# Three quarters of the first feed-forward product in 2x2 blocks, with seven block products for eight, and weight sums by accumulating DMAs

## The chip, the cores and the metric

The kernel runs on one core of a Trainium2 chip. The metric is device time in microseconds (us); the figure for the kernel before is the median of three runs. Five engines with a queue of instructions each matter here: PE (TensorE: matmuls, with weight loads of its own beside them), DVE (VectorE), ACT (ScalarE), POOL (GpSimd) and SP (SyncE, which here issues only DMAs). Each works through its own queue in order; an instruction that waits for another engine or for a transfer holds everything behind it on its engine.

## What is computed

Two layers run over 640 tokens (128 of a prompt, 512 of a sample) of width 1024. The layer's first part, a mixer of four branches, is not changed. Its second part is the feed-forward network:

```
h = _rmsnorm(x, g_pre_ffn) * (1 + sc2) + sh2
f = jnp.square(jax.nn.relu(h @ w_ff1)) @ w_ff2        # w_ff1: 1024 x 4096, w_ff2: 4096 x 1024
x = x + gt2 * _rmsnorm(f, g_post_ffn)
```

Shift, scale and gate (sh, sc, gt) come from `mod = SiLU(cond) @ w_ada + b_ada` for each layer, one set for the prompt and one for the sample.

## The kernel before

**Precision.** Every factor is split into a high part (rounded to the type that PE multiplies at full rate) and a low part (the rest), and a product is three matmuls: high by high, high by low, low by high (`mm3`). A raw weight tile `wr` (128x1024) is loaded by SP, its high part `wh` is a cast on ACT (L160), and its low part `wl` is a subtraction on DVE (L170) that needs `wh`. Each such tile is a unit; 132 units make a layer. `w_fetch` issues loads (three raw buffers), `w_pump` the casts up to three units ahead (four sets of `wh` and `wl`), `w_low` the subtractions.

**Stages.** The feed-forward network runs in four quarters of 1024 hidden columns. A quarter has two stages. In the first, 8 units of w_ff1 give 8 blocks of 128 hidden columns (tile `ff`): for each block and each half of the tokens (320), `ws_half` makes 8 x 3 = 24 matmuls of 320 columns, then ACT takes relu and square (L1121, L1122, the latter writes the high part `ghi`), and DVE squares and subtracts for the low part `glo` (L1123, L1124). In the second, `natural`, 8 units of w_ff2 multiply `ghi` and `glo` into the output `f` (tile `nat`), 240 matmuls of 512 columns, in two halves of four units; each unit serves all five tiles of 128 tokens.

**Order.** Nothing reorders the program: the code's order is the order of each engine's queue. After a chunk of matmuls, `tick(pe, dve)` adds the estimated PE time to a credit and takes the estimated DVE time off; while credit is left, it advances side jobs, the attention and convolution parts and `ada`, which makes the modulation vectors: per chunk (`ada_chunk`) eight loads `wa` issued by ACT into four buffers, 16 DVE operations on `acc` (L419, L421), two all-reduces over partitions on POOL (L433); for shift and scale, small POOL DMAs through DRAM follow (L443 `mrow`, L446 `mc`), for a gate, a product on DVE (L460). `tick` also lets one pending `wl` go (`w_low(1)`).

Of the kernel before, what the change touches and what calls it, by code (L numbers as in the profile page):

```python
# [12 lines left out]
L = 2  # L13
# [56 lines left out]
class Kernel:  # L70
# [35 lines left out]
    def add(self, name, gen, unit, steps):  # L106
        self.sides.append(Side(name, gen, self.l * N_UNITS + unit, steps))
# [31 lines left out]
    def w_init(self):  # L139
        self.w_dma = 0  # L140
        self.w_split = 0
        self.w_at = 0
        self.w_live = 0
        self.w_raw = {}
        self.w_raw_live = 0
# [3 lines left out]
    def w_pump(self, upto):
        nc = self.nc  # L150
        total = L * N_UNITS
        while self.w_split <= min(upto, total - 1) and self.w_live < N_SETS:
            i = self.w_split
            if i not in self.w_raw:
# [4 lines left out]
            lo = self.wp.tile([128, 1024], F32R, tag="wl", name=self.nm("wl"), bufs=N_SETS)  # L159
            nc.scalar.copy(hi, raw)  # L160
            self.w_set[i] = (hi, lo)
            self.w_late.append((i, raw, hi, lo))
            self.w_split += 1
            self.w_live += 1
# [11 lines left out]
    def w_fetch(self, upto):  # L176
        while self.w_dma <= min(upto, L * N_UNITS - 1):
            i = self.w_dma
            if self.w_raw_live >= N_RAW:
                break  # L180
            self.w_raw_live += 1
            raw = self.wp.tile([128, 1024], F32, tag="wr", name=self.nm("wr"), bufs=N_RAW)
            self.nc.sync.dma_start(raw, self.a["wu"][i])
            self.w_raw[i] = raw
            self.w_dma += 1

    def w_next(self):
# [3 lines left out]
        self.w_low(upto=i)  # L191
# [210 lines left out]
    def ada_chunk(self, l, ch, red):  # L402
# [4 lines left out]
        w = {}  # L407
        for k in range(-3, 8):
# [13 lines left out]
            yield 1.4  # L422
        if gate:
# [26 lines left out]
    def ada_gate(self, l, v, G):  # L450
        nc, a = self.nc, self.a
        for h in range(2):
# [3 lines left out]
            for c in range(2):  # L456
# [3 lines left out]
                nc.vector.tensor_tensor(G[c][:, s], red[c], gp, ALU.mult)  # L460
                yield 0.6
# [103 lines left out]
    def x_load(self, t, src, bufs=3):  # L565
# [5 lines left out]
    def natural(self, hi, lo, f, mode, ch=None):  # L571
# [5 lines left out]
        for n in range(2):  # L577
# [37 lines left out]
            for j in range(4):  # L615
                u, st = self.w_next()
                for t in range(NT):
# [5 lines left out]
                    self.tick(*NAT_TICK[j])  # L623
# [485 lines left out]

    def ffn(self, hi, lo, f, ch):  # L1110
        nc = self.nc
        for c in range(4):
# [31 lines left out]
    def run(self):  # L1144
# [3 lines left out]
        with tc.tile_pool(name="cp", bufs=1) as self.cp, tc.tile_pool(name="lp", bufs=1) as self.lp, \  # L1148
# [22 lines left out]
            for l in range(L):  # L1171
# [39 lines left out]
class Chain:  # L1211
# [180 lines left out]
```

## Time and profile before

| | |
|---|---|
| median of 3 runs (lowest to highest) | 2087.73 us (2086.01 to 2090.85) |
| profiled execution: its time; span from the first to the last instruction | 2086.46 us; 2084.5 us |
| PE busy | 2031.9 us (97%) |
| DVE busy | 1312.2 us (63%) |
| ACT busy | 786.5 us (38%) |
| POOL busy | 287.5 us (14%) |
| HBM read | 208.61 MB |
| mean granted clock of PE | 0.991 |

All times of the sum are taken from this one execution. Busy time counts what an engine executes; matmuls are pipelined, so PE can be busy and still be slower than its peak: the distance from one matmul's start to the next tells its real pace. Waits are found in the timeline as idle time before an instruction, with the engine that ended it. In part 2 of the page the span is cut in 40 slices; the feed-forward quarters lie at about 597 to 1057 us and 1623 to 2078 us.

### The profile page before, as it was taken

To read this page: it belongs to the slowest core of one execution; us is meant where nothing else is said; L and a number is where in the kernel's file an instruction comes from. 1 tells how busy PE (TensorE), PEld (TensorE's weight loads), DVE (VectorE), ACT (ScalarE), POOL (GpSimd) and SP (SyncE) were. 2 spreads that over 40 slices of the span, in tenths; PEclk is the share of its full clock that TensorE was granted. 3 is DMA by queue.
4 is the path that set the end of the run, shared out by engine and by line. 5 is a ranking of instruction groups with operands and counts; after the bars stand their busy time and mean duration, and the time that the engine had idled before them with its cause. 6 is when DMAs were issued, how large, how long until landed. Compare 5 with 4: busy or idle time off the path is not lost. (4 is left out here: it accounts for less than half of the span.)

```text
span 2084.5 us, 30672 instructions
## 1 busy us (share of the span) xinstructions
PE 2031.9 (97%) x12354; PEld 1884.3 (90%) x12354; DVE 1312.2 (63%) x2306; ACT 786.5 (38%) x1540; POOL 287.5 (14%) x214
## 2 busy tenths in 40 slices
PE   8999999999999999999999989999999999999998
PEld 4999999899889898989889989989998989989896
DVE  6777875687678385657776878667435863333344
ACT  5433445442353331313344334455324523223131
POOL 1302001013131123111240020100101211000000
PEclk9999999999999999999999999999999999999999
DMA  7331221233434244343534112112224342222232
GB/s 295 123 111 60 83 71 36 98 121 115 149 132 162 99 135 131 112 132 123 169 108 133 63 64 72 51 67 96 72 72 147 136 142 81 75 78 74 78 102 80
DMA packets 77934, 221.40 MB, mean 106 GB/s; under 512 B 11224, under 2 KB 12248, under 8 KB 77792
## 3 DMA queue, kind: packets, MB, share of 16 engines
q1 hardware_dynamic: 48736, 165.32, 23.0%
q10 hardware_dynamic: 27520, 54.03, 7.7%
q8 instruction: 96, 1.57, 0.3%
q0 software_dynamic: 1536, 0.10, 0.2%
q14 instruction: 46, 0.38, 0.1%
HBM read 208.61 MB, written 10.80 MB: 105 GB/s over the span
## 5 line engine op out<-in xcount | busy, mean ns | idle before, releaser
L170 DVE TENSOR_TENSOR wl<-wr,wh 128x1024 fp32r<-128x1024 f32 x264 | 346.6, 1316 | 211.4 <-ACT wh L160 210.2
L160 ACT CAST wh<-wr 128x1024 fp32r<-128x1024 f32 x264 | 274.1, 1045 | 367.8 <-PE nat L210 291.5
L213 PE MATMUL ff<-hlo,wh 128*128 128x320 f32 x1024 | 318.3, 311 | 4.0 <-DVE hlo L546 2.8
L212 PE MATMUL gp<-hhi,wh 128*128 128x320 f32 x1024 | 319.8, 312 | 0.8 <-ACT sg L1080 0.6
L214 PE MATMUL ff<-hhi,wl 128*128 128x320 f32 x1024 | 318.1, 311 | 1.3 <-DVE wl L170 1.3
L212 PE MATMUL ff<-hhi,wh 128*128 128x320 f32 x1024 | 318.2, 311 | 0.0
L213 PE MATMUL gp<-hlo,wh 128*128 128x320 f32 x1024 | 317.3, 310 | 0.0
L214 PE MATMUL gp<-hhi,wl 128*128 128x320 f32 x1024 | 317.2, 310 | 0.0
L209 PE MATMUL nat<-wl,ghi 128*128 128x512 f32 x640 | 252.5, 395 | 0.0
L210 PE MATMUL nat<-wh,glo 128*128 128x512 f32 x640 | 252.4, 394 | 0.0
L208 PE MATMUL nat<-wh,ghi 128*128 128x512 f32 x640 | 252.3, 394 | 0.0
L433 POOL PARTITION_ALL_REDUCE red<-acc x40 | 147.5, 3731 | 723.0 <-DVE acc L421 374.4
L213 PEld LDWEIGHTS ff<-hlo,wh 128*128 128x128 f32 x1024 | 193.4, 189 | 5.4 <-issue 3.4
L421 DVE SCALAR_TENSOR_TENSOR acc<-wa,silu_c,acc 128x512 f32<-128x512 f32 x280 | 195.9, 758 | 2.6 <-DMA wa<-in_wada_dram 2.6
L212 PEld LDWEIGHTS gp<-hhi,wh 128*128 128x128 f32 x1024 | 193.1, 189 | 2.4 <-ACT sg L1080 0.9
L214 PEld LDWEIGHTS ff<-hhi,wl 128*128 128x128 f32 x1024 | 193.6, 189 | 1.8 <-DVE wl L170 1.8
L213 PEld LDWEIGHTS gp<-hlo,wh 128*128 128x128 f32 x1024 | 193.0, 189 | 1.1
L212 PEld LDWEIGHTS ff<-hhi,wh 128*128 128x128 f32 x1024 | 193.4, 189 | 0.4
L214 PEld LDWEIGHTS gp<-hhi,wl 128*128 128x128 f32 x1024 | 192.9, 188 | 0.1
L1080 ACT ACTIVATE sg<-gp 128x320 f32<-128x320 f32 x128 | 55.4, 434 | 288.4 <-PE gp L214 244.3
L1123 DVE TENSOR_TENSOR r<-r 128x320 f32<-128x320 f32 x128 | 62.6, 489 | 156.7 <-ACT ghi L1122 156.5
L1121 ACT ACTIVATE r<-ff 128x320 f32<-128x320 f32 x128 | 55.9, 437 | 248.0 <-PE ff L214 239.8
(205 smaller groups left out, 3803.6 us busy)
## 6 DMA issues: line engine op xcount, KB each, us to landing
wr<-in_wu_dram SPq DMA_DIRECT2D x264, 512.0 KB, 3.2
wa<-in_wada_dram ACTq DMA_DIRECT2D x160, 256.0 KB, 3.0
wa<-in_wada_dram SPq DMA_DIRECT2D x16, 512.0 KB, 8.8
x<-x ACTq DMA_DIRECT2D x15, 512.0 KB, 2.7
x<-x SPq DMA_DIRECT2D x15, 512.0 KB, 6.0
x<-in_x_sample_dram SPq DMA_DIRECT2D x8, 512.0 KB, 9.9
gp<-in_g_post_dram ACTq DMA_DIRECT2D x16, 256.0 KB, 3.2
out_dram<-x SPq DMA_DIRECT2D x10, 256.0 KB, 2.0
```

What stands on the lines that cost most here:

```text
L160: nc.scalar.copy(hi, raw)
L170: self.nc.vector.tensor_tensor(lo, raw, r32(hi), ALU.subtract)
L208: mm(out, lhsT=xhi, rhs=whi, start=start, stop=False)
L209: mm(out, lhsT=xhi, rhs=wlo, start=False, stop=False)
L210: mm(out, lhsT=xlo, rhs=whi, start=False, stop=stop)
L212: mm(out, lhsT=whi, rhs=xhi, start=start, stop=False)
L213: mm(out, lhsT=whi, rhs=xlo, start=False, stop=False)
L214: mm(out, lhsT=wlo, rhs=xhi, start=False, stop=stop)
L421: nc.vector.scalar_tensor_tensor(acc[c], w[k], s, acc[c], ALU.mult, ALU.add)
L433: nc.gpsimd.partition_all_reduce(red[c], acc[c], 128, bass_isa.ReduceOp.add)
L1121: nc.scalar.activation(r, ps[:, :HALF], AF.Relu)
L1123: nc.vector.tensor_tensor(r, r, r, ALU.mult)
```

## The change

In the quarters 1 to 3 of both layers (not in quarter 0) `ffn` calls `ffn_pairs` in place of the 16 `ws_half`. The product is cut in 2x2 blocks: the 1024 input features in two halves, two neighbouring blocks of 128 hidden columns as a pair, and the tokens in two halves of 320. Seven block products of 4 x 3 = 12 matmuls of 320 columns (tile `ffp`) replace the eight of a pair; there are four pairs in a quarter, so 28 block products. They run in the order 7, 1, 2, 6, 5, 3, 4 (`PRODUCTS`).

Each block product has a weight of its own, 128x512, half a set: product 1 uses W11 and 5 uses W11+W12, made in buffer X; 7 uses W12+W22, 6 the same with W11 added, 4 the same with W21 added too, made one after the other in buffer Y; 2 and 3 use W21 and W22 (buffer Z, a `wr` tile). X and Y live in the four `wa` buffers. SP loads the first block; every further one is added by a DMA that POOL issues with `accum_op=ALU.add` (`w_sum`): Y+W22 as soon as Y is loaded (`w_fetch`), the others behind the `wl` subtraction that still reads the old sum (`w_low`). A pair has four such DMAs. Casts run five block products ahead (`w_pump(None, base + i + 5)`).

Sums of activations are made once a layer by `ffn_acts`, as a side job in the second stage of quarter 0: for four k, 14 DVE operations of 320 columns and 4 ACT casts. After the products, DVE and ACT combine the seven results in two tiles U and R (128x640), and make `ghi` and `glo` of them 640 wide.

While X or Y are alive, `ada_chunk` does not start (`yield 0`); before a quarter's first X is loaded, an open chunk is run to its end at one go (`while self.ada_open`). Then `natural` without a chain ticks by `FF_TICK`, the `x` tiles have four buffers, and the chain asks for its scale and shift later (`late`). In all, PE has 288 matmuls fewer (6 x 48) and POOL 96 DMAs more.

```
+FF0 = 68
+PRODUCTS = [(p, n) for p in range(4) for n in (7, 1, 2, 6, 5, 3, 4)]
+_ALL, _LEFT, _RIGHT = slice(0, 512), slice(0, 512), slice(512, 1024)
+SOURCE = {1: ("X", _ALL, "12"), 5: ("X", _ALL, None), 7: ("Y", _ALL, "11"), 6: ("Y", _ALL, "21"), 4: ("Y", _ALL, None),
+          2: ("Z", _LEFT, "keep"), 3: ("Z", _RIGHT, None)}
+FF_TICK = ((1.39, 0), (1.39, 0), (1.39, 0), (1.39, 0.7))
...
+    def w_pump(self, upto, part=None):
+        while self.w_split < len(self.parts):
+            i, c, key, rc, then = self.parts[self.w_split]
+            if (i > upto or key[0] != "u" and i > self.w_at) if part is None else self.w_split > part:
+                break
...
                 self.w_low()
-            self.w_fetch(i)
-            raw = self.w_raw.pop(i)
-            hi = self.wp.tile([128, 1024], F32R, tag="wh", name=self.nm("wh"), bufs=N_SETS)
...
+            nc.scalar.copy(hi, raw[:, rc])
...
     def w_low(self, n=None, upto=None):
 
         while self.w_late and (n is None or n > 0) and (upto is None or self.w_late[0][0] <= upto):
-            i, raw, hi, lo = self.w_late.pop(0)
+            _, key, raw, hi, lo, then = self.w_late.pop(0)
             self.nc.vector.tensor_tensor(lo, raw, r32(hi), ALU.subtract)
-            self.credit -= W_DVE
-            self.w_raw_live -= 1
-            self.w_fetch(i + N_RAW)
+            self.credit -= W_DVE if key[0] == "u" else W_DVE / 2
+            if then in ("11", "12", "21", "22"):
+                self.w_sum(key, then)
+            elif then != "keep":
+                del self.w_raw[key]
+                self.w_raw_live["wa" if key[0] in "XY" else "wr"] -= 1
+            self.w_fetch()
...
+    def block(self, u, b):
+        return self.a["wu"][u + int(b[1]) - 1][:, (int(b[0]) - 1) * 512:int(b[0]) * 512]
+    def w_sum(self, key, b):
+        self.nc.gpsimd.dma_start(self.w_raw[key], self.block(key[1], b), accum_op=ALU.add)
...
+    def w_fetch(self, upto=None):
+        while self.w_dma < len(self.loads) and (upto is None or self.w_dma <= upto):
+            key = src, u = self.loads[self.w_dma]
+            pool = "wa" if src in "XY" else "wr"
+            if self.w_raw_live[pool] >= (4 if src in "XY" else N_RAW):
                 break
-            self.w_raw_live += 1
-            raw = self.wp.tile([128, 1024], F32, tag="wr", name=self.nm("wr"), bufs=N_RAW)
-            self.nc.sync.dma_start(raw, self.a["wu"][i])
-            self.w_raw[i] = raw
+            if src == "X":
+                if self.pair_set.get(u, 0) > self.w_at + 1:
+                    break
+                while self.ada_open:
+                    next(self.side_ada.gen)
+            self.w_raw_live[pool] += 1
+            if pool == "wa":
+                raw = self.ap.tile([128, 512], F32, tag="wa", name=self.nm("wx"), bufs=4)
+                self.nc.sync.dma_start(raw, self.block(u, "11" if src == "X" else "12"))
+            else:
+                raw = self.wp.tile([128, 1024], F32, tag="wr", name=self.nm("wr"), bufs=N_RAW)
+                if src == "u":
+                    self.nc.sync.dma_start(raw, self.a["wu"][u])
+                else:
+                    for i, b in enumerate(("21", "22")):
+                        self.nc.sync.dma_start(raw[:, i * 512:i * 512 + 512], self.block(u, b))
+            self.w_raw[key] = raw
+            if src == "Y":
+                self.w_sum(key, "22")
             self.w_dma += 1
 
...
         acc = [self.ap.tile([128, 512], F32, tag=f"acc{c}", name=self.nm("acc"), bufs=1) for c in range(2)]
         gate = ch // 2 in (2, 5)
         w = {}
+        while any(k[0] in "XY" for k in self.w_raw):
+            yield 0
+        self.ada_open = True
...
-                    self.tick(*NAT_TICK[j])
+                    self.tick(*(NAT_TICK if ch else FF_TICK)[j])
...
+    def ffn_acts(self, hi, lo, S):
...
+            def fin(f, x):
+                nc.scalar.copy(x[0], f)
+                v(x[1], f, r32(x[0]), ALU.subtract)
+            for f, x, y in ((f1, a21, a22), (f3, a11, a21)):
+                v(f, x[0], y[0], ALU.subtract)
+                v(f, f, x[1], ALU.add)
+                v(f, f, y[1], ALU.subtract)
+                yield 1.5
+            v(f2, f1, a11[0], ALU.subtract)
+            v(f2, f2, a11[1], ALU.subtract)
+            fin(f1, s1)
+            fin(f3, s3)
+            yield 2.0
+            v(f4, a12[0], f2, ALU.add)
+            v(f4, a12[1], f4, ALU.add)
+            fin(f2, s2)
+            fin(f4, s4)
+            yield 2.0

+    def ffn_pairs(self, hi, lo, S, ghi, glo):
+        nc = self.nc
+        v = nc.vector.tensor_tensor
+        p, q = slice(0, HALF), slice(HALF, NTOK)
+        acts = {1: [(hi[k][:, p], lo[k][:, p]) for k in range(4)], 2: [(hi[k][:, p], lo[k][:, p]) for k in range(4, 8)],
+                4: [(hi[k][:, q], lo[k][:, q]) for k in range(4, 8)], 3: S[4], 5: S[1], 6: S[2], 7: S[3]}
+        base = self.set_part[self.w_at]
+        late = []
+        for i, (pr, n) in enumerate(PRODUCTS):
+            self.w_pump(None, base + i + 5)
+            self.w_low(upto=base + i)
+            wh, wl = [w[:, (i % 2) * 512:(i % 2) * 512 + 512] for w in self.w_set[self.w_at]]
+            if n == 7:
+                U, R = self.T("u"), self.T("r")
+                p7 = self.sdps("ffp")
+            ps = (p7 if n == 7 else self.mmps("ffp"))[:, :HALF]
+            for k in range(4):
+                c = slice(k * 128, k * 128 + 128)
+                self.mm3(ps, wh[:, c], wl[:, c], *acts[n][k], k == 0, k == 3)
+            if n == 1:
+                nc.scalar.copy(U[:, p], ps)
+            elif n == 2:
+                v(R[:, p], ps, U[:, p], ALU.add)
+            elif n == 6:
+                v(U[:, p], ps, U[:, p], ALU.add)
+                v(R[:, q], p7[:, :HALF], U[:, p], ALU.add)
+            elif n == 5:
+                v(U[:, q], ps, R[:, q], ALU.subtract)
+                v(U[:, p], ps, U[:, p], ALU.subtract)
+            elif n == 3:
+                v(U[:, p], ps, U[:, p], ALU.add)
+                nc.scalar.activation(U, U, AF.Relu)
+                nc.scalar.activation(U, U, AF.Square)
+                nc.scalar.copy(ghi[2 * pr + 1], U)
+                late.append((2 * pr + 1, U))
+            elif n == 4:
+                v(R[:, q], ps, R[:, q], ALU.add)
+                nc.vector.scalar_tensor_tensor(R, R, 0.0, R, ALU.max, ALU.mult)
+                nc.scalar.copy(ghi[2 * pr], R)
+                late.append((2 * pr, R))
+            if late and n in (1, 2):
+                j, x = late.pop(0)
+                v(glo[j], x, r32(ghi[j]), ALU.subtract)
+            if i % 2:
+                self.w_free(self.w_at)
+                self.w_at += 1
+            self.tick(1.76, 1.4)
+        for j, x in late:
+            v(glo[j], x, r32(ghi[j]), ALU.subtract)
+        self.credit = 0.0
+        self.w_pump(self.w_at + SPLIT_AHEAD - 1)
...
-            order = [(i, h) for i in range(8) for h in range(2)]
-            if c == 0:
-                order = [(i, 0) for i in range(4)] + [(i, 1) for i in range(4)] + order[8:]
+            order = [(i, 0) for i in range(4)] + [(i, 1) for i in range(4)] + [(i, h) for i in range(4, 8) for h in range(2)]
+            if c:
+                self.drain("sums")
+                self.ffn_pairs(hi, lo, S, ghi, glo)
...
+            if c == 0:
+                self.add("sums", self.ffn_acts(hi, lo, S), FF0 + 14, 12)
...
         if self.ab:
-            self.A, self.B = self.k.make_ab(*self.ab)
+            self.k.need(*self.ab)
+            self.A, self.B = self.k.make_ab(*self.k.res[self.ab])
```

How the order changes is shown at three places of quarter 1 of the first layer. First ACT. Before, in the middle of the quarter's first stage, relu (`r`), square (`ghi`) and the casts `wh` of whole units:

```order
L1121 ACTIVATE r_1305_7623<-ff1_1302_7591 128x320
L1122 ACTIVATE ghi_1260_7412<-r_1305_7623 128x320
L1121 ACTIVATE r_1307_7655<-ff1_1306_7628 128x320
L1122 ACTIVATE ghi_1260_7412<-r_1307_7655 128x320
L160 CAST wh_1308_7662<-wr_1278_7446 128x1024
L1121 ACTIVATE r_1312_7695<-ff1_1310_7665 128x320
L1122 ACTIVATE ghi_1261_7413<-r_1312_7695 128x320
L1121 ACTIVATE r_1314_7725<-ff1_1313_7700 128x320
```

Now, from pair 0 to pair 1 (`wx_1271` is Y and `wx_1270` X of pair 1, `wr_1272` its Z; `wh_1311` left by product 6; `u` is U, `ffp_1320` is product 1 of pair 1):

```order
L202 CAST wh_1305_7586<-wr_1272_7460 128x512
L202 CAST wh_1311_7629<-wx_1271_7457 128x512
L1251 ACTIVATE u_1297_7532<-u_1297_7532 128x640
L1252 ACTIVATE u_1297_7532<-u_1297_7532 128x640
L1253 CAST ghi_1278_7509<-u_1297_7532 128x640
L202 CAST wh_1311_7629<-wx_1270_7455 128x512
L1258 CAST ghi_1277_7508<-r_1298_7533 128x640
L202 CAST wh_1315_7669<-wr_1272_7460 128x512
L202 CAST wh_1315_7669<-wx_1271_7457 128x512
L1240 COPY u_1317_7672<-ffp_1320_7690 128x320
```

A cast from Y now stands ahead of the copy of product 1 out of PSUM (last two rows): the copy comes behind the cast for product 4, whose source is the third sum in Y.

DVE before, the same stretch:

```order
L170 TENSOR_TENSOR wl_1309_7663<-wr_1278_7446,wh_1308_7662 128x1024
L1123 TENSOR_TENSOR r_1312_7695<-r_1312_7695 128x320
L1124 TENSOR_TENSOR glo_1269_7421<-r_1312_7695,ghi_1261_7413 128x320
L1123 TENSOR_TENSOR r_1314_7725<-r_1314_7725 128x320
L1124 TENSOR_TENSOR glo_1269_7421<-r_1314_7725,ghi_1261_7413 128x320
L170 TENSOR_TENSOR wl_1316_7731<-wr_1291_7521,wh_1315_7730 128x1024
L1123 TENSOR_TENSOR r_1320_7763<-r_1320_7763 128x320
L1124 TENSOR_TENSOR glo_1270_7422<-r_1320_7763,ghi_1262_7414 128x320
```

DVE now (from the `wl` of product 6 of pair 1 to the `wl` of product 7 of pair 2, `wx_1308`):

```order
L210 TENSOR_TENSOR wl_1312_7630<-wx_1271_7457,wh_1311_7629 128x512
L1262 TENSOR_TENSOR glo_1286_7517<-u_1297_7532,ghi_1278_7509 128x640
L210 TENSOR_TENSOR wl_1312_7630<-wx_1270_7455,wh_1311_7629 128x512
L1242 TENSOR_TENSOR r_1318_7673<-ffp_1324_7711,u_1317_7672 128x320
L1262 TENSOR_TENSOR glo_1285_7516<-r_1298_7533,ghi_1277_7508 128x640
L210 TENSOR_TENSOR wl_1316_7670<-wr_1272_7460,wh_1315_7669 128x512
L1244 TENSOR_TENSOR u_1317_7672<-ffp_1325_7728,u_1317_7672 128x320
L1245 TENSOR_TENSOR r_1318_7673<-ffp_1319_7674,u_1317_7672 128x320
L210 TENSOR_TENSOR wl_1316_7670<-wx_1271_7457,wh_1315_7669 128x512
L1247 TENSOR_TENSOR u_1317_7672<-ffp_1331_7755,r_1318_7673 128x320
L1248 TENSOR_TENSOR u_1317_7672<-ffp_1331_7755,u_1317_7672 128x320
L210 TENSOR_TENSOR wl_1323_7709<-wx_1308_7605,wh_1322_7708 128x512
```

The `wl` from `wx` stand between the operations that combine the products; the last one, which frees the next Y for its second sum, comes behind both that use product 5 (`ffp_1331`).

POOL before, around the start of the same quarter: two reductions, then two more, then the small DMAs.

```order
L433 ISA red_1249_7327<-acc_1213_7068 128x512
L433 ISA red_1253_7347<-acc_1214_7069 128x512
L433 ISA red_1318_7746<-acc_1284_7498 128x512
L433 ISA red_1322_7781<-acc_1285_7499 128x512
L443 DMA mrow_1327_7816<-red_1318_7746 16x1x32
L443 DMA mrow_1328_7817<-red_1322_7781 16x1x32
L446 DMA mc_1282_7496<-mrow_1327_7816 128x4x1
L446 DMA mc_1282_7496<-mrow_1328_7817 128x4x1
```

POOL now, from the last two reductions before the quarter (`red`) through pair 0 into pair 1 (`wx_1268` is Y of pair 0, `wx_1271` Y of pair 1, `wx_1308` Y of pair 2, `wx_1267` and `wx_1270` are X of pairs 0 and 1):

```order
L504 ISA red_1263_7437<-acc_1225_7086 128x512
L504 ISA red_1264_7439<-acc_1226_7087 128x512
L225 DMA wx_1268_7449<-in_wu_dram 128x512
L225 DMA wx_1271_7457<-in_wu_dram 128x512
L225 DMA wx_1268_7449<-in_wu_dram 128x512
L225 DMA wx_1267_7447<-in_wu_dram 128x512
L225 DMA wx_1268_7449<-in_wu_dram 128x512
L225 DMA wx_1308_7605<-in_wu_dram 128x512
L225 DMA wx_1271_7457<-in_wu_dram 128x512
L225 DMA wx_1270_7455<-in_wu_dram 128x512
L225 DMA wx_1271_7457<-in_wu_dram 128x512
```

The first addition to Y of pair 2 stands ahead of the second one of pair 1, and the first addition of all behind the two reductions. The load of `wx_1308` that it adds to is issued by SP when the `wl` of product 4 of pair 0 has read that buffer.

## Rows read from the trace of the kernel before

**Rows 1.** The page, part 1: busy time, share of the span, instructions.
```profile
PE 2031.9 (97%) x12354; PEld 1884.3 (90%) x12354; DVE 1312.2 (63%) x2306; ACT 786.5 (38%) x1540; POOL 287.5 (14%) x214
```

**Rows 2.** Windows: us, then busy us of PE, PEld, DVE, ACT, POOL; clock, DMA share.
```profile
720.00:770.00 50.00, 50.00 (x343) 50.00 (x342) 37.09 (x56) 19.57 (x35) 10.50 (x6) 1.00 0.42 139
776.00:826.00 50.00, 50.00 (x216) 40.42 (x215) 29.30 (x40) 7.36 (x7) 19.46 (x12) 1.00 0.38 120
1745.00:1795.00 50.00, 50.00 (x343) 50.00 (x342) 22.42 (x36) 19.69 (x36) 0.00 (x0) 1.00 0.22 74
```

**Rows 3.** Tile ff from 700 to 790 us: durations, first and last start.
```profile
L212 PE MATMUL ff<-hhi,wh x128: 309/309/310, 716.3 to 772.1; 128*128 128x320 f32 x128
```

**Rows 4.** Single lines on DVE and ACT: durations in ns, min/median/max.
```profile
L746 DVE TENSOR_TENSOR ptl<-PT,pth x60: 675/684/693, 133.8 to 1463.2; 128x512 fp32r<-128x512 f32 x60
...
L1016 DVE SCALAR_TENSOR_TENSOR ml<-macc,mh x16: 814/826/2896, 468.4 to 1566.8; 128x640 fp32r<-128x640 f32 x16
...
L543 ACT CAST hhi<-h x24: 406/620/626, 27.3 to 1637.6; 128x512 fp32r<-128x512 f32 x20, 128x256 fp32r<-128x256 f32 x4
...
L1015 ACT ACTIVATE mh<-macc x16: 728/732/741, 467.3 to 1566.0; 128x640 fp32r<-128x640 f32 x16
...
L1037 ACT COPY sb<-sec x8: 403/426/429, 123.4 to 1168.4; 128x320 f32<-128x320 f32 x8
```

**Rows 5.** Timeline of ACT, then of DVE: start us, us, line, operation, idle before.
```profile
1742.31 1.05 ACT L160 CAST wh<-wr 128x1024 fp32r<-128x1024 f32 x1
...
1743.40 1.23 DVE L170 TENSOR_TENSOR wl<-wr,wh 128x1024 fp32r<-128x1024 f32 x1 [5.63 <-ACT wh L160]
...
1750.37 0.49 DVE L1124 TENSOR_TENSOR glo<-r,ghi 128x320 fp32r<-128x320 f32 x1
1750.77 0.69 DVE L460 TENSOR_TENSOR G<-red,gp 128x512 f32<-128x512 f32 x1
```

**Rows 6.** DMA issues: KB each, median us from issue to landing.
```profile
wr<-in_wu_dram SPq DMA_DIRECT2D x264, 512.0 KB, 3.2
wa<-in_wada_dram ACTq DMA_DIRECT2D x160, 256.0 KB, 3.0
...
mc<-mrow POOLq DMA_DIRECT2D x24, 2.0 KB, 3.2
```

**Rows 7.** Spread of the landing: line L412 (wa), then tile mc.
```profile
DMA to landing us min/median/max: 2.5/3.0/5.3
...
DMA to landing us min/median/max: 2.5/3.2/5.0
```

**Rows 8.** Timeline of POOL: start us, us, line, operation.
```profile
998.04 7.91 POOL L433 PARTITION_ALL_REDUCE red<-acc  x2 [24.56 <-DVE acc L421]
...
1009.67 0.79 POOL L446 DMA_DIRECT2D mc<-mrow  x1 [2.81 <-DMA mrow<-red]
```

**Rows 9.** Timeline of DVE beside another such reduction on POOL.
```profile
963.79 0.49 DVE L1124 TENSOR_TENSOR glo<-r,ghi 128x320 fp32r<-128x320 f32 x1
964.20 3.26 DVE L170 TENSOR_TENSOR wl<-wr,wh 128x1024 fp32r<-128x1024 f32 x1
```

**Rows 10.** Timeline of PE at and behind two short waits.
```profile
1624.44 0.38 PE L213 MATMUL ff<-hlo,wh 128*128 128x320 f32 x1 [1.27 <-DVE hlo L546]
1625.48 0.64 PE L214 MATMUL ff<-hhi,wl 128*128 128x320 f32 x1 [0.66 <-DVE wl L170]
...
1628.32 0.47 PE L212 MATMUL ff<-hhi,wh 128*128 128x320 f32 x1
...
1628.83 0.31 PE L214 MATMUL ff<-hhi,wl 128*128 128x320 f32 x1
```

**Rows 11.** Window behind these waits, columns as in Rows 2.
```profile
1625.60:1628.60 3.00, 3.00 (x12) 3.00 (x13) 2.93 (x6) 0.06 (x1) 0.55 (x1) 0.50 0.63 190
```

**Rows 12.** The page, part 5: the sums of the modulation.
```profile
L421 DVE SCALAR_TENSOR_TENSOR acc<-wa,silu_c,acc 128x512 f32<-128x512 f32 x280 | 195.9, 758 | 2.6 <-DMA wa<-in_wada_dram 2.6
```

More of the change, by code (lines that the diff above doesn't have):

```diff
@@ L106, in add @@
     def add(self, name, gen, unit, steps):
-        self.sides.append(Side(name, gen, self.l * N_UNITS + unit, steps))
+        self.sides.append(Side(name, gen, self.set0[self.l] + unit, steps))
     def drain(self, *names):
@@ L139, in w_init @@
     def w_init(self):
+        self.parts, self.loads, self.set_part, self.set0, self.pair_set = [], [], [], [], {}
+        for l in range(L):
+            self.set0.append(len(self.set_part))
+            u = 0
+            while u < N_UNITS:
+                g = l * N_UNITS + u
+                if u < FF0 + 16 or (u - FF0) % 16:
+                    self.set_part.append(len(self.parts))
+                    self.parts.append((len(self.set_part) - 1, slice(0, 1024), ("u", g), slice(0, 1024), None))
+                    self.loads.append(("u", g))
+                    u += 1
+                    continue
+                for i, (p, n) in enumerate(PRODUCTS):
+                    if i % 2 == 0:
+                        self.set_part.append(len(self.parts))
+                        if i == 0:
+                            self.pair_set[g] = len(self.set_part) - 1
+                    src, cols, then = SOURCE[n]
+                    at = (i % 2) * 512
+                    self.parts.append((len(self.set_part) - 1, slice(at, at + 512), (src, g + 2 * p), cols, then))
+                self.loads += [(src, g + 2 * p) for p in range(4) for src in ("X", "Y", "Z")]
+                u += 8
+        self.set_part.append(len(self.parts))
         self.w_dma = 0
@@ L144, in w_init @@
         self.w_raw = {}
[L145 removed]
+        self.w_raw_live = {"wr": 0, "wa": 0}
         self.w_late = []
         self.w_set = {}
[L149 removed]
+        self.ada_open = False
+    def w_pump(self, upto, part=None):
         nc = self.nc
[L151 to L154, printed above, removed]
[L155 to L162 removed]
+        while self.w_split < len(self.parts):
+            i, c, key, rc, then = self.parts[self.w_split]
+            if (i > upto or key[0] != "u" and i > self.w_at) if part is None else self.w_split > part:
+                break
+            if i not in self.w_set:
+                if self.w_live >= N_SETS:
+                    break
+                self.w_set[i] = [self.wp.tile([128, 1024], F32R, tag=n, name=self.nm(n), bufs=N_SETS) for n in ("wh", "wl")]
+                self.w_live += 1
+            if key not in self.w_raw:
+                self.w_low()
+            while key[0] in "XY" and any(x[1] == key for x in self.w_late):
+                self.w_low(1)
+            self.w_fetch()
+            raw = self.w_raw[key]
+            hi, lo = [w[:, c] for w in self.w_set[i]]
+            nc.scalar.copy(hi, raw[:, rc])
+            self.w_late.append((self.w_split, key, raw[:, rc], hi, lo, then))
@@ L422, in ada_chunk @@
             yield 1.4
+        self.ada_open = gate
         if gate:
@@ L1110, in ffn @@
     def ffn(self, hi, lo, f, ch):
         nc = self.nc
+        S = {n: [] for n in range(1, 5)}
         for c in range(4):
```

33 lines of the change are left out of this document (22 added, 11 removed).

## The prediction

> **What bounds the kernel now.** I read the busy times first: PE is busy for 97% of the span, DVE for 63% [rows 1]. Busy is not yet bound, so next come windows inside the stages that change. In the first stage of a quarter 341 to 343 matmuls fit in 50 us, without a gap and at full clock; in the second stage 215 or 216 [rows 2]. So matmuls of 320 columns start 0.1466 us apart (50/341), those of 512 columns 0.2325 (50/215). A first stage begins at 716.3 and its last three matmuls at 772.1, with 3 x 128 = 384 matmuls [rows 3]: 56.3 us, which is 384 x 0.1466. So the stage is bound by the number of matmuls alone. DVE has 37 of 50 us there while modulation is made, 22 when it is not, ACT 20 [rows 2]. Then I read single operations [rows 4, 5], transfers [rows 6, 7], POOL [rows 8, 9] and the clock [rows 10, 11], because the change brings waits that this stage doesn't have.
>
> **What goes and what comes.** 48 matmuls fewer in each of six stages: 48 x 0.1466 = 7.0 us, 42 us in all; the floor of a stage is 28 x 12 x 0.1466 = 49.3 us. On DVE 8 `wl` (1.23 us) and 32 operations of 320 columns (0.49) go, 25.5 us; 28 half `wl` (0.68, as the operation of that shape in rows 4) and per pair seven operations of 320 and three of 640 (0.83) come: 19.0 + 4 x 5.9 = 42.7 us [rows 4, 5]. On ACT 28 half casts (0.62), and per pair a copy (0.43) and four of 640 (0.73): 31 us. Both would fit in 49.3 us, so neither is bound by its load. They are bound by their order, and that is what I price.
>
> **The chain in a pair.** Let x be the time from the end of the `wl` that frees Y to the moment at which the cast of the new sum can start: POOL's issue, transfer, landing. In ACT's order the cast for product 4 (third sum in Y) stands ahead of the copy of product 1. DVE's sums, and behind them the `wl` for 3, for 4, and for product 7 of the next pair, wait for that copy, and the next Y's second sum waits for this last `wl`. So one pair's third sum, which itself waits for the second, holds the next pair's second: a closed loop with two transfers in a row. POOL's order adds a third: Y+W22 of the pair after next stands ahead of the second sum of the next pair, and waits for a load into the buffer that product 4's `wl` has just freed. From the end of the `wl` for 4 to the same a pair later:
> load of Y, 2.7 us (256 KB land in 2.5 at the fastest, 3.0 in the middle [rows 6, 7]); POOL's issue of the addition, 0.8 [rows 8]; x; cast for 6 and its `wl`, 0.62 + 0.68 and two hand-overs of 0.04 (1743.36 to 1743.40 [rows 5]), 1.4; x; cast for 4 and the copy, 0.62 + 0.43, 1.1; on DVE a sum, a 640-wide `glo`, `wl` for 3, two sums, `wl` for 4, 0.49 + 0.83 + 0.68 + 0.98 + 0.68 less 5 x 0.09 overlap (1750.37 + 0.49 against 1750.77 [rows 5]), 3.2. Together 9.2 + 2x, where PE needs 84 x 0.1466 = 12.3.
>
> The quarter: the first pair's `wl` for 6 ends about 2.0 after the start (last evacuation 0.69 [rows 5], two half `wl`), then x, 1.1, and 2.5 on DVE: 5.6 + x. Two loops with the load in them: 18.4 + 4x. The last pair has none: 1.5 to its second sum, x, 1.4, x, 1.1, 1.8 on DVE, 5.8 + 2x; then PE still has 3.2 of block products 3 and 4. A stage takes **33.0 + 7x**, not under 49.3. It is even with 56.3 at x = 3.3.
>
> **The unknown x.** No transfer before adds to its target, and none from POOL is of this size. From below: a plain 256 KB load lands at the earliest 2.5 after its issue, and so does POOL's 2 KB `mc` [rows 7]. From above: `mc` has taken 5.0 and a `wa` load 5.3 [rows 7]; with the target read as well, 6. Between them: `mc` has 3.2 in the middle, and what 256 KB add is half of the 512 KB load (3.2) less the 256 KB load's fastest (2.5), 0.7 [rows 6, 7]. 3.2 + 0.7 = **3.9**, which I take: it is nearest to POOL's own row. Reading the target speaks for more (another 0.7), a quiet queue for less; traffic in these stages doubles (2 MB for 1 MB per pair), on queues that are busy for 0.22 to 0.42 before [rows 2]. At 3.9 a stage takes 60.3: 4.0 more, six times 24 us.
>
> **The starts.** Before quarter 1 of each layer a whole chunk of modulation and its two reductions stand ahead of the first `wl` on DVE and the first addition on POOL. The last unit's set comes free at half of the second stage (240 x 0.2325 = 55.8, so 27.9); cast and `wl` to 30.8, eight activation sums to 35, the chunk's loads 3 and seven steps of two operations (0.76 [rows 12]) to 47 or 48, the reductions 7.9 [rows 8]: 55.3. Y lands at 59.2, is cast at 59.9: PE starts about 4 late, and the second sum (`wl`, x, cast, `wl`) is 6 after the start where the sum above has 2: another 4. Twice 8 is 16. In quarters 2 and 3 of layer 0 the chunk runs earlier; the reductions end 5.6 before the start, the `wl` for 6 comes 5 after it, 3 late: 6 in all. In layer 1 there is no modulation left then. Beside a reduction DVE is held too: a `wl` of 1.23 takes 3.26 [rows 9]; the starts' estimate has that hidden, since DVE there waits for the same reductions. The 56 activation sums of a layer (27 us on DVE) lie in a second stage in which DVE has some 29 of 50 us [rows 2]; what they push back is in the start's 8.
>
> **The clock.** After waits of 1.27 and 0.66 us PE ran at the lower level: 12 matmuls in 3.0 us, so some 0.26 apart, at a granted clock of 0.50, before the higher one came back between 1628.3 and 1628.8 [rows 10, 11]. The 3.4 us from 1625.4 on at half pace cost 1.7. Inside a pair the chain hides it: from the release of 3 to the next pair's 6, PE has about 8.5 to do and the chain takes 9.7. Behind the last wait of a quarter nothing hides it: 6 x 1.7 = 10.
>
> **The sum.** 24 + 16 + 6 + 10 = 56 us on the profiled execution's own 2086.5: 2142.5. The median is 1.3 above that execution; I predict **2143**. As a rule in x: the total changes by 50x - 139 us, of which nought is at 2.8. Edits put at nothing: the fourth `x` buffer, the later request for scale and shift (hidden by a second stage in which DVE has 20 us to spare), the modulation chunks that move out of the first stages: if those no longer fit beside the second stages and the mixer, each costs up to its 11 us.
>
> The Trainium skill, page "DMA: Bandwidth & Descriptors", section "Anatomy of one DMA — SWDGE (gpsimd) path", fits a transfer from POOL as 2.0 us plus bytes over 436 GB/s. By it 256 KB take an estimated 2.6, and the sum would be rival A. This trace does not agree with its 2.0: 2 KB took 2.5 to 5.0 from POOL [rows 7].
>
> **Rivals.**
> A. The additions land like the fastest load, x = 2.6. Against it: only the fastest rows are so quick, and they move or read less. Then a stage takes 51.2, 5.1 less: -31, starts 2 x 5.4 + 2 x 0.4 = 12, no clock loss: **2068**. It decides below x = 2.8. Chance 0.14. By the fit of the Trainium skill above this is what would happen.
> B. The waits bind nowhere, x at or under 2.3 (say because the additions start moving before POOL's issue ends): -42 and 10 for the starts, **2055**. No row has a landing like that for a load. Chance 0.05.
> C. The additions queue behind the loads, x = 5: a stage takes 68, **2197**. For it: the spread of rows 7, and that 2 MB share the queues in a pair. Chance 0.15. The Trainium skill, same page, section "Issuing engines are not separate DMA queues", has all transfers interleave on the same 16 engines; the spread agrees.
> D. PE stays at the lower clock through these stages, because every pair has waits longer than those of rows 10: 28 x 12 x 0.26 = 87 us a stage, 31 more, **2271**. Against it: in 3.4 us without a wait it came back [rows 10]. Chance 0.03.
> That the change doesn't do what it says isn't one: 288 matmuls are gone from PE's order.
>
> **The numbers.** The forecast, x from 2.9 to 4.6, has 0.63: 2092 to 2178 (50x - 139 = 6 and 91). Faster by over 0.2%, about the smallest difference that a measurement tells from none: A and B, 0.19. Within it, x close to 2.8, off the forecast's lower end: 0.04. Slower: the rest of the forecast, C and D, 0.77. The range of 8 in 10 reaches down to A (2066) and up past C (2203): outside are B, D and the tails.
>
> **What would show it.** Right: PE's idle time before block products 6, 5 and 3, put down to `wh` and `wl` of the new tiles; ACT's casts from `wx` waiting for POOL's DMAs, and right behind them the copy of product 1 late by microseconds; first stages of some 60 us; landings of about 4 on POOL; the first stages of quarter 1 starting late. Wrong in size if landings are under 3; wrong in kind if the matmuls of a first stage follow each other at 0.147 without waits, or if PE waits for DVE at work rather than for transfers.

## The result, and the profile after

The changed kernel takes 2204.58 us (median of 4 runs, 2203.39 to 2206.72), the kernel before 2089.28 in the same comparison: ratio 1.0555, 95% interval 1.0537 to 1.0573. It is slower, as forecast, but by 115 us where 55 were forecast, and just above the range. The profiled execution has a span of 2201.6 us, 117.1 more than before.

Part 1 of the page answers to [rows 1]: PE has 288 matmuls fewer and a smaller share of the span; its busy time is longer all the same, which is due to its clock (below).

```profile
PE 2052.8 (93%) x12066; PEld 1877.5 (85%) x12066; DVE 1443.5 (66%) x2586; ACT 832.0 (38%) x1620; POOL 368.1 (17%) x310
```

Windows over the six changed stages, and over the two stretches ahead of the first quarter of each layer; columns as in [rows 2].

```profile
723.30:800.50 77.20, 62.58 (x337) 59.14 (x338) 38.62 (x66) 30.00 (x52) 13.22 (x15) 0.86 0.49 101
856.30:930.90 74.60, 59.50 (x338) 54.89 (x337) 37.97 (x66) 26.48 (x45) 12.36 (x15) 0.91 0.48 100
986.40:1060.60 74.20, 59.28 (x338) 54.79 (x337) 37.87 (x66) 26.42 (x45) 12.18 (x15) 0.91 0.49 101
1813.60:1889.30 75.70, 63.56 (x337) 59.49 (x338) 38.84 (x66) 29.85 (x52) 13.18 (x15) 0.84 0.49 103
1945.00:2012.80 67.80, 55.05 (x337) 50.85 (x336) 36.08 (x64) 25.27 (x43) 10.56 (x12) 0.97 0.49 105
2068.50:2138.80 70.30, 57.22 (x338) 54.03 (x337) 37.60 (x65) 26.45 (x45) 10.56 (x12) 0.93 0.47 102
...
717.30:723.30 6.00, 0.00 (x0) 0.00 (x0) 0.00 (x0) 0.65 (x2) 0.04 (x1) 0.84 0.77 209
1808.20:1813.60 5.40, 0.03 (x1) 0.03 (x1) 0.04 (x1) 0.69 (x2) 0.00 (x0) 0.69 0.81 225
```

The stages take 439.8 us together, 73.3 each, where six of 56.3 made 338: 102 of the 117 us. Another 11 are the two starts, in which PE stands still; 4 lie outside. PE was idle for 12 to 15 us in each stage, and its granted clock fell to 0.84 to 0.97, so that its busy time is well over the floor of 49.3. DVE has 39 us or less: no engine is at its load. What PE waited for in the stage of quarter 3 of layer 0 (us, times, longest) are the new tiles and the copy of product 1:

```profile
PE ffp L281 <- DVE wl L210: 5.0, 7, 1.3
PE ffp L279 <- ACT u L1240: 5.0, 4, 3.0
PE ffp L279 <- ACT wh L202: 4.6, 3, 2.6
```

The loop between two pairs, in quarter 3 of layer 0: POOL, then ACT, then DVE (start us, us, line, operation, idle before).

```profile
1025.20 2.63 POOL L225 DMA_DIRECT2D wx<-in_wu_dram  x3 [10.92 <-DVE r L1256]
1032.79 0.85 POOL L225 DMA_DIRECT2D wx<-in_wu_dram  x1 [4.95 <-DVE wl L210]
...
1031.04 0.62 ACT L202 CAST wh<-wx 128x512 fp32r<-128x512 f32 x1 [11.06 <-DMA wx<-in_wu_dram]
...
1036.88 0.62 ACT L202 CAST wh<-wx 128x512 fp32r<-128x512 f32 x1 [1.39 <-DMA wx<-in_wu_dram]
1037.41 0.42 ACT L1240 COPY u<-ffp 128x320 f32<-128x320 f32 x1
...
1021.13 0.68 DVE L210 TENSOR_TENSOR wl<-wx,wh 128x512 fp32r<-128x512 f32 x1
...
1031.69 0.69 DVE L210 TENSOR_TENSOR wl<-wx,wh 128x512 fp32r<-128x512 f32 x1 [5.62 <-ACT wh L202]
...
1037.86 0.49 DVE L1242 TENSOR_TENSOR r<-ffp,u 128x320 f32<-128x320 f32 x1 [2.58 <-ACT u L1240]
...
1040.53 0.68 DVE L210 TENSOR_TENSOR wl<-wx,wh 128x512 fp32r<-128x512 f32 x1
```

And the landings in the chain of waits, in the same stage from 1013 us on (start us, us):

```profile
1013.43 4.03 DMA wx<-in_wu_dram
...
1025.78 5.24 DMA wx<-in_wu_dram
...
1043.01 3.93 DMA wx<-in_wu_dram
...
1048.78 4.03 DMA wx<-in_wu_dram
```

Read the three queues as one circle (product 4's half weight is called 4, and so on). The `wl` for 4 (1021.13) frees Y; SP loads into it at 1021.88; POOL adds W22 at 1025.20 and only then (0.58 later) issues the second sum of the next pair. That lands at 1031.02; cast, `wl`, third sum (1032.79), landed at 1036.80; cast, copy of product 1 right behind it, DVE's sums, and at 1040.53 the next `wl` for 4, 19.4 us after the first. PE needs 12.3. The trace puts POOL's idle time before 1025.20 down to a sum of DVE's that ended 0.6 us earlier; that it is the load, the second experiment (e2) shows.

### The profile page after: what moved, and what is told of

Its sections match the earlier page's. It is cut to its first block, busy times and chain, and to the rows that moved or that the text cites. A ratio compares the mean times of both kernels' runs of the same rounds, so it can differ in the third digit from the quotient of the medians.

```text
span 2201.6 us, 30950 instructions
## 1 busy us (share of the span) xinstructions
PE 2052.8 (93%) x12066; PEld 1877.5 (85%) x12066; DVE 1443.5 (66%) x2586; ACT 832.0 (38%) x1620; POOL 368.1 (17%) x310
## 3 DMA queue, kind: packets, MB, share of 16 engines
q0 software_dynamic: 15360, 25.27, 7.6%
## 4 chain that ended last, share of the span: by engine, by line
PE 28%; DVE 7%; DMA 7%; issue 7%; ACT 3%; POOL 2%; SPq 0%; POOLq 0%; ACTq 0%; DVEq 0%
DMA wx<-in_wu_dram 6%; PE nat L275 3%; PE nat L276 3%; PE nat L277 3%; PE gp L281 2%; PE gp L280 2%; PE gp L279 2%; DVE wl L210 2%; PE sec L279 1%; PE sec L280 1%; PE sec L281 1%; PE bp L279 1%; PE bp L280 1%; PE bp L281 1%; ACT wh L202 1%
## 5 line engine op out<-in xcount | busy, mean ns | idle before, releaser
L210 DVE TENSOR_TENSOR wl<-wr,wh 128x1024 fp32r<-128x1024 f32 (+1 forms) x264 | 317.3, 1204 | 101.8 <-ACT wh L202 100.5
L202 ACT CAST wh<-wr 128x1024 fp32r<-128x1024 f32 (+1 forms) x264 | 253.6, 969 | 223.2 <-PE nat L277 128.9
L202 ACT CAST wh<-wx 128x512 fp32r<-128x512 f32 x120 | 71.8, 618 | 392.4 <-DMA wx<-in_wu_dram 354.1
L225 POOL DMA_DIRECT2D wx<-in_wu_dram x96 | 85.0, 998 | 437.0 <-DVE wl L210 199.8
L281 PE MATMUL ffp<-hhi,wl 128*128 128x320 f32 x384 | 130.9, 341 | 24.9 <-DVE wl L210 24.9
L210 DVE TENSOR_TENSOR wl<-wx,wh 128x512 fp32r<-128x512 f32 x120 | 81.9, 684 | 108.5 <-ACT wh L202 108.5
L279 PE MATMUL ffp<-hhi,wh 128*128 128x320 f32 x384 | 130.8, 341 | 22.0 <-ACT u L1240 22.0
L277 PEld LDWEIGHTS nat<-wh,glo 128*128 128x128 f32 x640 | 120.2, 188 | 28.8
L276 PEld LDWEIGHTS nat<-wl,ghi 128*128 128x128 f32 x640 | 120.2, 188 | 27.8
L275 PEld LDWEIGHTS nat<-wh,ghi 128*128 128x128 f32 x640 | 120.2, 188 | 27.8
```

Source lines behind the costliest of these rows:

```text
L202: nc.scalar.copy(hi, raw[:, rc])
L225: self.nc.gpsimd.dma_start(self.w_raw[key], self.block(key[1], b), accum_op=ALU.add)
L275: mm(out, lhsT=xhi, rhs=whi, start=start, stop=False)
L276: mm(out, lhsT=xhi, rhs=wlo, start=False, stop=False)
L277: mm(out, lhsT=xlo, rhs=whi, start=False, stop=stop)
L279: mm(out, lhsT=whi, rhs=xhi, start=start, stop=False)
```

## The experiments

A mean of x is taken over the 24 second sums (POOL's issue to the start of the cast) and the 24 third sums (end of the `wl` for 6 to the start of the cast for 4) of a trace. Ratios are to the kernel before, run beside each; what is won or lost in us is counted from the changed kernel's 2204.58. Code is cut where a line is `...`.

**No additions.**

```diff
 def w_sum(self, key, b):
-    self.nc.gpsimd.dma_start(self.w_raw[key], self.block(key[1], b), accum_op=ALU.add)
+    return
```

> Leaves out all 96 additions (POOL issues none of them, so five of seven block products use a single block of the weights); order and all other work stay. Theory (the stages are long because casts wait for additions, x): without x nothing binds but PE, a first stage is 49.3 to 51 us instead of 67.8 to 77.1, the starts keep some 6 to 12 us of waits for modulation: 2050 to 2070. Rival (DVE's and ACT's 28 half casts, half low parts and the sums are too much or in a bad order by themselves): stages of 56 or more, 2100 or more.

Measured: 2046.82, ratio 0.9809 (0.9794 to 0.9824), 3 us below the theory's range; in its trace a stage (quarter 2 of layer 0) is at the floor:

```profile
820.00:869.30 49.30, 49.30 (x338) 49.26 (x337) 37.74 (x65) 25.22 (x42) 0.00 (x0) 1.00 0.24 77
```

So the half casts, the half low parts, the sums and the moved modulation cost nothing: PE's -42 is all that is left (-40 measured), and the waits ahead of the first quarters are gone too. All of the loss is the additions. This run leaves out their traffic too, so it does not tell the adding from the bytes.

**The order: the addition for the pair after next later; the copy earlier; both.**

```diff
 # e2: in w_fetch, for pairs 2 and 3; y_sums(), which issues w_sum(key, "22"), runs right behind the sum "12" of X
-                self.w_sum(key, "22")
+                self.y_new.append(key)
...
 # e3: in ffn_pairs
-            self.w_pump(None, base + i + 5)
+            self.w_pump(None, base + i + (4 if n == 1 else 5))
```

> POOL issues the addition Y+W22 for the pair after next behind the addition X+W12 of the next pair instead of ahead of the next pair's second Y sum. Theory: the load of Y (3.4 us from the end of the third block's low part to POOL's issue), the issue (0.6) and the burst (second sum 5.3 instead of 4.45) leave the loop: the two middle loops of a stage fall from 19.4 to 20.9 to about 16.0, which the last pair already has: 2 x 3.4 to 4 x 6 = 41 to 48 us less, 2155 to 2165. Rival (the additions are bound by the traffic or by POOL, not by their order): same as the changed kernel, 2195 to 2205.

Measured: 2180.99, ratio 1.0444 (1.0424 to 1.0465): 24 us won, half of what was expected. In the middle pairs the second sum now starts 0.4 after the `wl` for 7, in the changed kernel 2.4 or more, so the load did hold it; but it lands later:

```profile
1955.25 1.89 POOL L231 DMA_DIRECT2D wx<-in_wu_dram  x2 [9.30 <-DVE u L1263]
...
1963.32 0.62 ACT L206 CAST wh<-wx 128x512 fp32r<-128x512 f32 x1 [11.70 <-DMA wx<-in_wu_dram]
```

8.07 us from issue to cast, where the changed kernel has 5.3 in the same place. It meets the loads that it had waited for: POOL's queue and SP's (q1), while the second sum was under way, in this run (1955.25 to 1963.29; packets, MB, share of 16 engines):

```profile
q1 hardware_dynamic: 490, 1.13, 48.3%
q0 software_dynamic: 335, 0.63, 45.2%
```

> ACT copies block product 1 out of PSUM ahead of the cast for product 4 instead of behind it. Theory: DVE's sums and the low parts for 3 no longer wait for the third sum of Y; the loop keeps the load, two landings, two casts and low parts: about 16.5 for 19.4 to 20.9, the last pair 13 for 16, the first 12.4 for 14.6: per stage about 11 less, 2125 to 2150. Rival (the wait moves to the low part of 4, which stands ahead of the next pair's 7, and nothing is won): 2190 to 2205.

Measured: 2151.38, ratio 1.0315 (1.0299 to 1.0331): 53 us won, 1 less than the theory's range. The copy behind the cast for 4 was on the loop.

> Both edits of the two runs beside it. Theory: from the end of one third low part to the next: low part of 7 0.7 to 1.4, 4.45, cast and low part 1.34, 4.5, cast and low part 1.3: 12.3 to 13.0 against PE's 12.3; a stage of 52 to 55 instead of 73: 2075 to 2100, near the kernel before. Rival (each edit takes the same wait, the gains do not add): no better than the better of the two, 2125 to 2165.

Measured: 2130.70, ratio 1.0210 (1.0193 to 1.0227): 74 us won, 24 + 53 = 77 apart. The gains add, so the rival's reason falls, though the time lies in its range: the theory missed by 31 even at the upper end of its range. In the trace (a landing in the chain of waits, then the timeline of ACT):

```profile
1921.02 7.26 DMA wx<-in_wu_dram
...
1928.30 0.62 ACT L206 CAST wh<-wx 128x512 fp32r<-128x512 f32 x1 [9.30 <-DMA wx<-in_wu_dram]
1928.83 0.73 ACT L1264 ACTIVATE u<-u 128x640 f32<-128x640 f32 x1
1929.59 0.74 ACT L1265 ACTIVATE u<-u 128x640 f32<-128x640 f32 x1
...
1932.66 0.41 ACT L1253 COPY u<-ffp 128x320 f32<-128x320 f32 x1
```

I had overlooked that ACT's work on the last pair's products, and behind it the copy, stands behind the cast for 6 as well; and this sum takes 7.3 us to land.

**The price of x: overwriting instead of adding; adding half.**

```diff
 # e5: in w_sum
-..., self.block(key[1], b), accum_op=ALU.add)
+..., self.block(key[1], b))
 # e6: in w_sum
-    self.nc.gpsimd.dma_start(self.w_raw[key], self.block(key[1], b), accum_op=ALU.add)
+    self.nc.gpsimd.dma_start(self.w_raw[key][:, 0:256], self.block(key[1], b)[:, 0:256], accum_op=ALU.add)
```

> Leaves out the adding: the same 96 transfers, same queue, size and place, that overwrite their target instead of adding to it (so the sums are missing from the weights). Theory 1 (adding costs a read of the target): a lone landing falls from 4.0 us to about 3.2, what a 2 KB transfer of POOL has in the middle; at 50 us of total for 1 us of x that is 40 less, 2155 to 2175. Theory 2 (the landing is POOL's fixed cost and the bytes, adding is free): 2195 to 2210.

Measured: 2138.78, ratio 1.0249 (1.0230 to 1.0269): 66 us less. Theory 1 is right in kind and had the adding too cheap.

> Each addition covers 256 of the 512 columns, 128 KB for 256 (leaves out the other half of every sum). Theory 1 (most of a landing is fixed cost): 0.2 to 0.4 us less when alone, more in a burst (0.5 to 1): 2165 to 2190. Theory 2 (bytes carry the landing, adding at a low rate): a lone landing of 3 or less, 2130 to 2160.

Measured: 2147.54, ratio 1.0288 (1.0272 to 1.0305): 57 us less, in the range of theory 2: the bytes, when added, carry much of a landing. Its other sign, a lone landing of 3 or less, did not come: the third sums land in 3.3 in the middle, where the changed kernel has 4.0 and e5 3.2. POOL's line L225 in the changed kernel, in e5 and in e6 (before, POOL's `mc` had 2.5/3.2/5.0 [rows 7]):

```profile
DMA to landing us min/median/max: 3.6/4.6/7.2
```

```profile
DMA to landing us min/median/max: 2.8/3.3/5.2
```

```profile
DMA to landing us min/median/max: 3.0/3.4/5.7
```

And POOL's queue (packets, MB, share of 16 engines' span), in the same order:

```profile
q0 software_dynamic: 15360, 25.27, 7.6%
```

```profile
q0 software_dynamic: 9216, 25.27, 3.9%
```

```profile
q0 software_dynamic: 15360, 12.69, 4.3%
```

Same bytes in the changed kernel and in e5, twice the time of the DMA engines: 7.6 against 3.9%. Without additions that queue has 0.3%, so one addition of 256 KB takes, on average, 16 engines' time for (7.6 - 0.3)% x 2201.6 / 96 = 1.7 us, an overwriting transfer for 0.8. Adding costs 0.9 of their time, close to the 0.8 between two lone landings (4.0, as above, and 3.2 in the middle of e5's third sums).

Means of x: 4.92 in the changed kernel, 3.92 in e6, 3.66 in e5. The prediction's rule, 50x - 139 on 2087.8, gives 2195, 2145, 2132; measured were 2205, 2148, 2139.

**Both edits of the order, and overwriting.**

> Both edits of the order together with transfers that overwrite instead of adding (the sums are missing from the weights). With both edits and adding, the loop still took 17.2 us a pair, 7.3 of it the landing of the second sum, which had company from other additions and loads. Theory (adding in company is what stretches that landing): without adding it lands in 3.3 to 4.5, the loop is 13.2 to 14.5, a stage 53 to 57: 2075 to 2100. Rival (the traffic as such stretches it, adding or not): the second sum lands in 5.5 or more and the time is 2115 to 2130.

Measured: 2099.25, ratio 1.0048 (1.0033 to 1.0063): the time is in the theory's range, at its upper end, 31 us below the same order with adding. But its step did not come as told: in the twelve middle pairs the second sum lands in 4.9 to 6.3, where adding has 6.3 to 7.7 (e4); the middle, 5.7, is the rival's sign. The longest:

```profile
1892.06 6.32 DMA wx<-in_wu_dram
```

So both count, the adding (about 1 us of such a landing) and the company of loads and other transfers; the kernel is still not faster than before.

**The sums on an engine.** All four blocks of a pair are in SBUF: W11 in X, W12 in Y, W21 and W22 in Z.

```diff
     def w_sum(self, key, b):
-        self.nc.gpsimd.dma_start(self.w_raw[key], self.block(key[1], b), accum_op=ALU.add)
+        u = key[1]
+        x, y, z = [self.w_raw.get((n, u)) for n in "XYZ"]
+        add = self.nc.gpsimd.tensor_tensor      # e8: self.nc.vector.tensor_tensor
+        if b == "22":
+            add(y, y, z[:, 512:1024], ALU.add)
+        elif b == "11":
+            add(y, y, x, ALU.add)
+        elif b == "12":
+            add(x, y, z[:, 512:1024], ALU.subtract)
+        else:
+            add(y, y, z[:, 0:512], ALU.add)
...
```

In both, the first sum (W22 into Y) is made in `w_pump` right ahead of the cast that needs it, when Z is loaded.

> The same sums, computed by POOL from the blocks that are in SBUF anyway (12 + 22 from Z, + 11 from X, + 21 from Z; the sum 11 + 12 as the second sum of Y less 22); no transfer for an addition, so 1 MB of loads per pair instead of 2 MB. Theory (x is all that holds PE back): x is then the length of one POOL operation of 128x512, between DVE's 0.7 and the 3.6 of POOL's reduction of that shape: at 1.5 or less the stages are bound by PE, 2047 to 2065; at 2.5 2065 to 2080. Rival (POOL and DVE slow each other in SBUF, or the loads of Z come too late): 2090 or more.

Measured: 2084.43 (10 runs), ratio 0.9986 (0.9975 to 0.9998), above the theory's range. In the stages all is as expected (50 to 54 us), but the first sum of a quarter stands on POOL behind the reductions, and PE starts 2 to 10 us late in four of the six. The rival has a part in it: 40 of the 120 `wl` from X and Y took 1.2 to 1.8 us, each of them beside an operation of POOL's; with the sums on DVE (e8) none did (ns, min/median/max, e7 then e8):

```profile
L217 DVE TENSOR_TENSOR wl<-wx,wh x120: 676/682/1792, 726.8 to 2019.8; 128x512 fp32r<-128x512 f32 x120
```

```profile
L217 DVE TENSOR_TENSOR wl<-wx,wh x120: 679/682/692, 718.0 to 1983.2; 128x512 fp32r<-128x512 f32 x120
```

> The same sums from the same tiles, computed by DVE. Theory: DVE has 42.7 us of work in a stage of 49.3 and gets 16 x 0.7 more: 54, bound by DVE's load, 5 more per stage than without sums: 2070 to 2085. Rival (no handing over between engines, so PE alone binds): 2047 to 2060.

Measured: **2052.66**, ratio 0.9840 (0.9822 to 0.9858): faster than both kernels, by 35 and 152 us. Its page's group of the first sum, and windows over two of its stages:

```profile
L236 DVE TENSOR_TENSOR wx<-wx,wr 128x512 f32<-128x512 f32 x24 | 16.4, 685 | 4.9 <-DMA wr<-in_wu_dram 4.9
```

```profile
825.20:874.40 49.20, 49.20 (x337) 49.20 (x336) 45.66 (x78) 24.95 (x42) 0.00 (x0) 1.00 0.24 77
930.00:979.30 49.30, 49.30 (x338) 49.29 (x337) 45.73 (x78) 24.93 (x42) 0.00 (x0) 1.00 0.24 77
```

My theory had DVE bound at 54; it has 45.7, since the changed kernel's DVE has 36 to 39 in a stage, not the 42.7 of the prediction. The rival was right: in these stages PE alone binds.

## Why the prediction was wrong

**The mechanism was right.** PE waits for DVE's and ACT's new tiles, ACT's casts wait for POOL's transfers, and the copy of product 1 stands behind them. The loop, piece by piece (forecast, then measured from 1021.81 to 1041.20): Y's load until POOL issues 2.7, 3.4; issue ahead 0.8, 0.6; second sum 3.9, 5.3; cast and `wl` 1.4, 1.3; third sum 3.9, 4.5; rest of the cast and copy 1.1, 0.9; DVE 3.2, 3.4. Together 17.0, 19.4: two of the 2.4 us are the two x.

**The step that failed is "The unknown x": 3.9 taken, 4.9 measured.** For a lone landing 3.9 was close (the third sums land in 3.9 to 4.9, in the middle 4.0), but by luck: two errors cancelled. The adding was left out: the prediction named 0.7 for reading the target and then set a "quiet queue" against it; e5 shows 0.8 for it in a lone landing. And 0.7 was put in for 256 KB, though e5's third sums, which move the same 256 KB without adding, land in 3.2 in the middle, no later than `mc` with 2 KB [rows 7].

What made x longer are two other things. First, the hand-overs, 0.4 of the 1.0: from the end of a `wl` to POOL's issue 0.4 us (1032.38 to 1032.79), more where POOL is held (below), and 0.02 to 0.1 from landing to cast; I had defined x with them and valued it without. Second, company (other transfers under way at the same time), 0.5 of the 1.0: in the twelve middle pairs, where the second sum is issued some 0.6 behind one addition and some 0.6 ahead of another, it lands in 5.2 to 6.6, in ten of the twelve other pairs in 3.9 to 4.3. The last 0.1 is the lone landing's own. By the rule of 50 us per microsecond of x, 1.0 more is 50 of the 62 us missed; its slope is measured at 52 (e5) and 57 (e6).

The rival whose number came true is C, x = 5 and 2197, which had 0.15. Its reason, queueing behind the loads, is a part at most. In the second pair of a quarter the second sum has additions beside it and next to no loads (SP's queue takes under 1% of the engines' time), and still lands in 5.2 to 5.7; in the third pair, with loads beside it too, in 5.2 to 6.6. POOL's queue while the second sum at 1006.31 was under way (to 1011.64; SP's queue moved nothing then):

```profile
q0 software_dynamic: 359, 0.67, 78.0%
```

The Trainium skill, page "DMA: Bandwidth & Descriptors", section "Anatomy of one DMA — SWDGE (gpsimd) path", would give an estimated 2.6 for 256 KB. The traces do not agree: overwriting transfers from POOL (e5) took 2.8 at the fastest and 3.3 in the middle, adding ones 3.6 and 4.6.

**The starts**: 4 late was forecast for PE in quarter 1, 6.0 and 5.4 came. POOL, in front of quarter 1 of layer 0, with reductions like those of [rows 8], and at the start of quarter 3:

```profile
709.64 6.75 POOL L504 PARTITION_ALL_REDUCE red<-acc  x2 [56.51 <-DVE acc L499]
716.27 1.07 POOL L225 DMA_DIRECT2D wx<-in_wu_dram  x1
723.42 2.67 POOL L225 DMA_DIRECT2D wx<-in_wu_dram  x3 [6.09 <-DMA wr<-in_wu_dram]
...
988.73 0.81 POOL L517 DMA_DIRECT2D mc<-mrow  x1 [2.25 <-issue]
991.68 0.77 POOL L517 DMA_DIRECT2D mc<-mrow  x1 [2.14 <-issue]
992.44 0.94 POOL L225 DMA_DIRECT2D wx<-in_wu_dram  x1
```

The first addition, issued at 716.27 as the reductions end, landed only 6.3 later (722.55), again an x. In quarters 2 and 3 of layer 0 I had priced the reductions but not the two `mc` transfers behind them: POOL is idle for 2.1 to 2.3 ahead of each (on what, the profile does not tell), with the third sum, whose `wl` ended at 989.77, in line until 992.44. The third sums of these two first pairs took 7.9 and 7.6 and stand in the mean of x.

**The clock**: 10 was forecast, 1.7 behind the last wait of each stage, from [rows 10, 11]. In quarter 3 of layer 0, then in quarter 2 of layer 1:

```profile
1055.70:1060.50 4.80, 4.80 (x22) 4.80 (x23) 4.76 (x8) 1.06 (x2) 0.00 (x0) 0.64 0.46 128
2009.47:2012.80 3.33, 3.33 (x22) 3.33 (x23) 3.29 (x7) 0.00 (x0) 0.00 (x0) 1.00 0.49 157
```

22 matmuls in 4.8 us, 1.6 over 22 x 0.1466: as forecast, and so it is in five of the six stages. In the sixth they take 3.3 us at full clock, behind a wait of the same 1.30 us; why, no run tells. Inside the stages the loop above has no piece in which DVE or ACT waits for PE, so the lower level costs nothing in it. Rival D, the lower level throughout, is refuted by clocks of 0.84 to 0.97.

**DVE's load** was set too high (42.7 for 36 to 39), which changed nothing here: its sum left out that an operation starts some 0.09 before the one ahead of it ends, which the loop's sum took from [rows 5].

**The pieces together.** The profiled execution (2203.4) lies 61 us above the sum (2142.5). With each x as the trace has it, the prediction's pieces can be laid beside the six stages. The 42 x in them take 46 us more than at 3.9. The rest of the twelve loops takes 8 more: 0.3 to 0.5 in ten of them, where the load of Y is 0.7 longer and other pieces shorter, and 2.5 and 1.8 in the first loops of quarters 1 and 3 of layer 0, where Y's load until POOL issues takes 5.5 and 4.8. PE's two late starts take 3 more, and 4 lie outside of the stages. The rest (the lateness of the first pairs, the last pairs, the clock) came, each, to within 2 us of what was forecast.

## What to carry to other kernels

Price a transfer by what it does, not by its bytes alone, from the moment that its cause ends, and with what moves beside it. Where the same latency stands several times in a loop, an error in it counts as often (here 50 times), so work the forecast out at both ends of its range, and measure it first if that can be done. Before moving arithmetic into transfers, look whether the operands are in SBUF anyway: in each stage, sixteen operations of 0.69 us on an engine with room made the kernel faster, where 16 transfers of 4 to 5 us had made it slower. In an in-order queue, look at everything behind an instruction that waits; freeing one of several chains moved the wait to the next here (e4).

## What the runs showed of the hardware that was not expected

An adding transfer takes twice the DMA engines' time of an overwriting one of the same bytes (7.6 against 3.9% of the span), in 144 packets instead of 80 ((15360 - 1536)/96 and (9216 - 1536)/96), and its issue holds POOL for 0.88 us where the other's takes 0.54. Of three issued some 0.6 apart, the second takes more than 1 us longer to land than a lone one (5.2 to 5.7 for 4.0), with next to no load beside them. POOL adds 128x512 in 1.3 to 1.7 us, DVE in 0.69:

```profile
L242 POOL TENSOR_TENSOR wx<-wx,wr 128x512 f32<-128x512 f32 x24 | 40.4, 1684 | 45.1 <-issue 41.0 <-DMA wr<-in_wu_dram 4.0
...
L238 POOL TENSOR_TENSOR wx<-wx,wx 128x512 f32<-128x512 f32 x24 | 31.7, 1323 | 143.5 <-DVE wl L217 143.5
```

The Trainium skill, page "GPSIMD Engine Reference", section "4.1 Engine selection", calls POOL about half as fast for additions of two operands; these rows agree.
